# A decoder trunk on one core: layer 0's gates, sums and outputs stored by blocks of 128 tokens, and queries and keys asked for earlier in the code

## The chip, the cores and the metric

The kernel runs on one core of a Trainium2 chip. The metric is device time in microseconds (us): the median of several runs of the whole program. The engines are named as in the profile: PE (matrix multiply), DVE, ACT and POOL (elementwise work), and SP, which here only issues DMAs. SP and POOL each issue theirs in order from one queue, and the DMAs move data between DRAM and the core's SBUF.

## What is computed

Two transformer layers over one sequence of 2048 tokens of width 1024, in float32. Layer 0 has 16 heads, 8 of multi-head latent attention (MLA) and 8 of forgetting attention (FoX); both are causal softmax attention over all earlier tokens. Layer 1 is sliding-window attention and is not touched. Cut to what matters here:

```python
def even_mixer(x, w_in, ..., w_out, pos):
    h = x @ w_in
    cq, ckv, k_pe, fq, fk, fv, f_logit, gate = _split(h, EVEN_SIZES)
    ...
    o = jnp.concatenate([_merge(o_mla), _merge(o_fox)], axis=-1)
    return (o * jax.nn.silu(gate)) @ w_out

x = layer_norm(ALPHA * x + even_mixer(x, ...), ln_g, ln_b)
```

The kernel divides by the softmax sum late: attention leaves an undivided output, and the reciprocal of the sum of each head and token is multiplied in together with the gate.

## The kernel before, in words

Products keep float32 accuracy by splitting each operand into a high and a low part (`split_ps` L74, `split_sb` L78) and multiplying three times (`mm3` L85). The program is written with a tile library: each engine's order comes from its scheduler, which may place an instruction earlier than the code does, as soon as the buffer that it writes comes free. A buffer pool with `bufs=2` hands out two buffers in turn.

**Phase 1** (L186) computes layer 0's projections for four chunks of 512 tokens. `feature_tile` makes the SiLU gate, 128 channels by 512 tokens at a time, and stores it into `g1` in DRAM (L352), laid out as channel by token. Queries, keys and values go to DRAM as well.

**Phase 2** (L483) walks 16 heads by 4 chunks of queries, MLA and FoX in turn. `produce` (L509) loads the queries of one head and chunk (tiles `q0`, `q1`, pool `qpool`, two buffers; L519 to L528), multiplies them with the keys `ka` and `kb` that `load_head` (L457) brought, and takes the exponentials into `p`. It stores the reciprocal sums into `rd`, laid out as head by token (L565). `consume` (L567) transposes `p` on PE, splits it, multiplies by the values and stores the head's 64 rows into `og1[c]` (L591). The main loop (L667) interleaves `produce` of one step with `consume` of the step before. In the last step `prefetch` (L638) loads what layer 0's output product needs first: weights, the attention outputs of token blocks 0 and 1, and their gates and reciprocal sums, both blocks in one piece (L649). POOL multiplies them (L652, L654).

**Phase 3** (L778) makes the output product, the residual and the norm, one block of 128 tokens at a time, 16 blocks. `load_og` (L794) prepares a block:

```python
gt, rb = (bits(v[:]) for v in hl)            # the two tiles that later hold the split parts oh, ol
load_gate(gt, rb, t * 128, 128)
og = opool.tile([128, KB, 128], F32, name="og", bufs=1)
nc.sync.dma_start(out=og[:], in_=og1[t // 4][:, :, tok(t % 4)])
nc.gpsimd.tensor_tensor(out=og[:], in0=og[:], in1=gt, op=OP.mult)
nc.vector.tensor_tensor(out=og[:], in0=og[:], in1=rb, op=OP.mult)
return split_og(og[:], hl)
```

`load_gate` (L477) brings the gate (512 KB, into `oh`) and, for even and odd heads apart, the reciprocal sums (256 KB each, into `ol`), each copied out to 64 partitions. The tile `og` has one buffer, `oh` and `ol` have three each, and the residual tile `z` has five. `out_block` (L718) multiplies a prepared block on PE (48 matmuls into `py`, L727 to L729), adds the residual, and after every second block queues a norm (`finish` L766: ACT L768, then L771 and L772 on POOL for the first block and on DVE for the second, then the store to `x1` from POOL's queue). Near the end of phase 3 layer 1's first input is turned on PE (L146) and split (L76).

Of the kernel before, what the change touches and what calls it, by code (L numbers as in the profile page):

```python
# [17 lines left out]
T = 2048  # L18
# [21 lines left out]
def decoder_trunk(ctx, tc, x, x_t, w_lat, w_main, w_u, g_lat, b_f, w_out1, ln1,  # L40
# [20 lines left out]
    rd = dram.tile([16, T], F32, name="rd")  # L61
    g1 = dram.tile([D, T], F32, name="g1")
    og1 = [dram.tile([128, KB, 512], F32, name=f"og1_{c}") for c in range(4)]
# [7 lines left out]
    def bits(ap):  # L71
        return ap.bitcast(F32)
# [113 lines left out]
    def phase1(late):  # L186
# [145 lines left out]
        def feature_tile(n, m, chunk, xT, w):  # L332
# [14 lines left out]
            else:  # L347
# [4 lines left out]
                queue.dma_start(out=g1[p * 128:(p + 1) * 128, tcs], in_=sg[:])  # L352
# [124 lines left out]
    def load_gate(gt, rb, t0, n):  # L477

        nc.sync.dma_start(out=gt, in_=g1[:, t0:t0 + n].rearrange("(k p) t -> p k t", p=128))
        for s_ in range(2):  # L480
            nc.sync.dma_start(out=rb[s_ * 64:s_ * 64 + 64], in_=rd[:].rearrange("(k s) t -> s k t", s=2)[s_:s_ + 1, :, t0:t0 + n].broadcast_to([64, KB, n]))

    def phase2(ctx, kpool):  # L483
# [24 lines left out]

        def produce(n, c, st):  # L509
# [9 lines left out]
            q0 = qpool.tile([128, 512], F32R, name="q0")  # L519
            if mla:  # L520
                q1 = qpool.tile([128, 512], F32R, name="q1")
                for i, q in enumerate((q0, q1)):
                    nc.sync.dma_start(out=bits(q[0:64, :]), in_=qn[i][h, :, tcs])
                    for s_ in range(2):
                        nc.sync.dma_start(out=bits(q[64 + s_ * 16:80 + s_ * 16, :]), in_=qr[i][s_][h, :, tcs])
            else:
                nc.sync.dma_start(out=bits(q0[0:64, :]), in_=qf[0][h, :, tcs])
                nc.sync.dma_start(out=bits(q0[64:128, :]), in_=qf[1][h, :, tcs])  # L528
# [36 lines left out]
            nc.sync.dma_start(out=rd[h if mla else 8 + h, tcs].rearrange("(j p) -> p j", p=128), in_=rec[:])  # L565

        def consume(n, c, P):  # L567
# [18 lines left out]
            def finish(po):  # L586
                t2 = qpool.tile([64, 512], F32, name="t2")
                nc.scalar.copy(out=t2[:], in_=po[64:128, :])
                nc.vector.tensor_tensor(out=t2[:], in0=po[0:64, :], in1=t2[:], op=OP.add)  # L589
                queue = nc.gpsimd if (n, c) == (15, 3) else nc.sync  # L590
                queue.dma_start(out=og1[c][(hd % 2) * 64:(hd % 2) * 64 + 64, hd // 2, :], in_=t2[:])  # L591
# [45 lines left out]

        def prefetch():  # L638
# [9 lines left out]
            gts, rbs = (ppool.tile([128, T], F32, name="p")[:].rearrange("p (k q) -> p k q", k=KB) for _ in range(2))  # L648
            load_gate(gts, rbs, 0, 256)  # L649
            for t in range(2):  # L650
                nc.sync.dma_start(out=wout["og"][t], in_=og1[0][:, :, tok(t)])
            nc.gpsimd.tensor_tensor(out=gts, in0=gts, in1=rbs, op=OP.mult)  # L652
            for t in range(2):
                nc.gpsimd.tensor_tensor(out=wout["og"][t], in0=wout["og"][t], in1=gts[:, :, tok(t)], op=OP.mult)  # L654
            for steps, k, tag in ((PRE[0], 7, "vv"), (PRE[1], 4, "ka"), (PRE[2], 6, "kb")):
                for _ in range(steps):
                    yield 1
                wo_split(k, tag, raw[k], True)
            for _ in range(99):
                yield 1  # L660
# [6 lines left out]
        for n, c in todo + [(None, None)]:  # L667
            st = []
            gens = []
            if (n, c) == (15, 3):  # L670
                r3, r5 = wo_load(kpool.tile([128, T], F32, name="cb"), 3, 5)
            if n is None:
# [105 lines left out]
    def phase3(stack4, kpool, wout):  # L778
        with ExitStack() as ctx:
# [14 lines left out]
            def load_og(t):  # L794
                hl = parts()
                gt, rb = (bits(v[:]) for v in hl)
                load_gate(gt, rb, t * 128, 128)
                og = opool.tile([128, KB, 128], F32, name="og", bufs=1)
                nc.sync.dma_start(out=og[:], in_=og1[t // 4][:, :, tok(t % 4)])
# [462 lines left out]
```

## Time and profile before

| | us |
|---|---|
| three runs | 2655.42, 2666.89, 2667.24 |
| their median | 2666.89 |
| the profiled execution, its own time | 2674.29 |
| its span, first to last instruction | 2672.5 |
| PE busy in it | 2471.1 (92%) |
| DVE, ACT, POOL busy | 1531.1, 1172.7, 707.0 |

The profile is of one execution. A busy time says how long an engine had work in hand, not whether that work was on the path that sets the end. So it is read with the chain of work that ended last, with the waits of PE, and with windows: the same columns for one stretch of the span at a time, so that a stage stands by itself.

### The profile page before, as it was taken

To read this page: it belongs to the slowest core of one execution; us is meant where nothing else is said; L and a number is where in the kernel's file an instruction comes from. 1 tells how busy PE (TensorE), PEld (TensorE's weight loads), DVE (VectorE), ACT (ScalarE), POOL (GpSimd) and SP (SyncE) were. 2 spreads that over 40 slices of the span, in tenths; PEclk is the share of its full clock that TensorE was granted. 3 is DMA by queue.
4 is the path that set the end of the run, shared out by engine and by line. 5 is a ranking of instruction groups with operands and counts; after the bars stand their busy time and mean duration, and the time that the engine had idled before them with its cause. 6 is when DMAs were issued, how large, how long until landed. Compare 5 with 4: busy or idle time off the path is not lost.

```text
span 2672.5 us, 36349 instructions
## 1 busy us (share of the span) xinstructions
PE 2471.1 (92%) x12885; PEld 2050.3 (77%) x12885; DVE 1531.1 (57%) x3002; ACT 1172.7 (44%) x2409; POOL 707.0 (26%) x694
## 2 busy tenths in 40 slices
PE   8999999999999999999999787659999999999997
PEld 7898888987788887888877665437888887777775
DVE  5442264317787877777777643345633644777775
ACT  3121222217676866777676501011121115566663
POOL 2010011101222221222222333232321321356555
PEclk9999999999999999999999888879999999999998
DMA  6574346654556665454554558854444653566563
GB/s 204 177 251 143 106 152 235 202 167 62 95 93 93 83 114 86 83 111 79 97 84 83 115 151 170 151 129 156 142 138 141 177 154 100 150 150 165 155 155 103
DMA packets 298566, 360.91 MB, mean 135 GB/s; under 512 B 55920, under 2 KB 202352, under 8 KB 293776
## 3 DMA queue, kind: packets, MB, share of 16 engines
q1 hardware_dynamic: 294224, 343.51, 53.6%
q0 software_dynamic: 4160, 15.08, 1.5%
q8 instruction: 102, 1.67, 0.3%
q14 instruction: 80, 0.66, 0.2%
HBM read 240.20 MB, written 118.29 MB: 134 GB/s over the span
## 4 chain that ended last, share of the span: by engine, by line
PE 68%; DMA 17%; DVE 5%; POOL 3%; ACT 3%; issue 3%; SPq 1%; POOLq 0%; DVEq 0%; ACTq 0%
PE pm L91 11%; PE pm L89 11%; PE pm L90 10%; PE pt L604 6%; DMA og<-og 5%; PE S L547 4%; PE S L548 4%; PE po L581 3%; PE po L582 3%; DMA kb<-kf 3%; DMA q<-qr 3%; DMA q<-qf 2%; PE S L1061 2%; PE py L727 2%; PE S L550 2%
## 5 line engine op out<-in xcount | busy, mean ns | idle before, releaser
L76 DVE TENSOR_TENSOR tl<-pt,th 128x512 fp32r<-128x512 f32 (+3 forms) x672 | 400.7, 611 | 128.4 <-ACT th L75 125.2
L89 PE MATMUL pm<-xh,w 128*128 128x512 f32 x1088 | 428.7, 394 | 7.5 <-DVE z L734 5.6
L75 ACT CAST th<-pt 128x512 fp32r<-128x512 f32 (+3 forms) x672 | 340.4, 524 | 203.2 <-PE pt L604 168.1
L91 PE MATMUL pm<-xh,w 128*128 128x512 f32 x1088 | 425.9, 392 | 0.0
L90 PE MATMUL pm<-xl,w 128*128 128x512 f32 x1088 | 425.6, 391 | 0.0
L604 PE MATMUL pt<-ident,p 128*128 128x128 f32 x2176 | 348.0, 280 | 4.0 <-DVE tl L76 3.9
L561 ACT ACTIVATE p<-p,mx 128x128 f32<-128x128 f32 (+15 forms) x256 | 309.0, 1207 | 29.3 <-DVE mx L558 27.5
L604 PEld LDWEIGHTS pt<-ident,p 128*128 128x128 f32 x2176 | 271.8, 145 | 58.6 <-DVE tl L76 7.3
L547 PE MATMUL S<-ka,q 96*128 96x512 f32 (+5 forms) x640 | 253.4, 396 | 29.6 <-DMA q<-qf 11.5
L581 PE MATMUL po<-th,vv 128*128 128x512 f32 (+2 forms) x640 | 278.0, 434 | 0.6 <-DVE t L589 0.4
L82 POOL TENSOR_SCALAR w<-w_raw 128x1024 fp32r<-128x1024 f32 (+3 forms) x88 | 98.5, 1132 | 581.3 <-PE pm L91 418.8
L89 PEld LDWEIGHTS pm<-xh,w 128*128 128x128 f32 x1088 | 205.0, 188 | 49.5 <-issue 7.3
L582 PE MATMUL po<-tl,vv 128*128 128x512 f32 (+2 forms) x640 | 238.3, 373 | 0.0
L91 PEld LDWEIGHTS pm<-xh,w 128*128 128x128 f32 x1088 | 204.7, 188 | 42.9
L90 PEld LDWEIGHTS pm<-xl,w 128*128 128x128 f32 x1088 | 204.9, 188 | 41.6
L609 POOL TENSOR_SCALAR th<-tf 128x512 fp32r<-128x512 f32 x96 | 59.4, 618 | 668.8 <-ACT tf L608 363.8
L548 PE MATMUL S<-kb,q 96*128 96x512 f32 (+5 forms) x640 | 234.4, 369 | 0.0
L83 DVE TENSOR_TENSOR w<-w_raw,w 128x1024 fp32r<-128x1024 f32 (+3 forms) x89 | 138.6, 1572 | 130.4 <-POOL w L82 127.4
L558 DVE CUSTOM_DVE_ANT_0 p<-S,zm 128x1024 f32<-128x1024 f32 (+7 forms) x128 | 123.7, 967 | 104.4 <-PE S L550 103.4
L547 PEld LDWEIGHTS S<-ka,q 128*128 128x128 f32 (+1 forms) x640 | 124.5, 194 | 54.5 <-issue 23.3
L1062 DVE CUSTOM_DVE_ANT_0 p<-S,bm,nsk 128x256 f32<-128x256 f32 x256 | 117.7, 477 | 71.8 <-PE S L1061 69.7
L1064 ACT ACTIVATE p<-p,mx 128x256 f32<-128x256 f32 x256 | 129.0, 505 | 66.2 <-DVE mx L1062 65.7
(249 smaller groups left out, 4771.0 us busy)
## 6 DMA issues: line engine op xcount, KB each, us to landing
w_raw<-in_w_main_dram SPq DMA_DIRECT2D x40, 512.0 KB, 5.2
w_raw<-in_w_odd_dram SPq DMA_DIRECT2D x36, 512.0 KB, 4.5
vd<-s_v SPq DMA_DIRECT2D x64, 256.0 KB, 2.7
vv<-vd SPq DMA_DIRECT2D x16, 1024.0 KB, 10.6
qs<-hl SPq DMA_DIRECT2D x64, 256.0 KB, 3.5
qt<-qs SPq DMA_DIRECT2D x64, 256.0 KB, 5.3
ka<-kf SPq DMA_DIRECT2D x16, 512.0 KB, 9.4
kb<-kf SPq DMA_DIRECT2D x16, 512.0 KB, 9.0
```

The lines of the kernel that those rows point to most:

```text
L75: nc.scalar.copy(out=hi, in_=src)
L76: nc.vector.tensor_tensor(out=lo, in0=src, in1=bits(hi), op=OP.subtract)
L83: nc.vector.tensor_tensor(out=lo, in0=src, in1=bits(hi), op=OP.subtract)
L89: nc.tensor.matmul(ps, lhsT=ah, rhs=bh, start=(i == 0), stop=False)
L90: nc.tensor.matmul(ps, lhsT=ah, rhs=bl, start=False, stop=False)
L91: nc.tensor.matmul(ps, lhsT=al, rhs=bh, start=False, stop=(i == n - 1))
L547: nc.tensor.matmul(dst, lhsT=q0[ds, js], rhs=ka[ds, ks_], start=True, stop=False)
L548: nc.tensor.matmul(dst, lhsT=q0[ds, js], rhs=kb_[ds, ks_], start=False, stop=not (mla or diag))
L561: nc.scalar.activation(out=p[:, 0:L], in_=p[:, 0:L], func=AF.Exp, scale=-1.0, bias=acc[:], accum_out=su[:, j:j + 1])
L581: nc.tensor.matmul(po[0][:, q_:512], lhsT=vv[:, kb, :], rhs=th[:, k, q_:512], start=(kb == 0), stop=False)
L582: nc.tensor.matmul(po[0][:, q_:512], lhsT=vv[:, kb, :], rhs=tl[:, k, q_:512], start=False, stop=(kb == c * 4 + 3))
L604: nc.tensor.transpose(out=pt[:, k, :], in_=P[j][:, kk:kk + 128], identity=ident[:])
```

## The change

The layouts of `rd`, `g1` and `og1` in DRAM become block by block: all that a block of 128 tokens needs lies together, 4 KB in a row for each partition (for `rd`, 4 KB for the even heads and 4 KB for the odd heads). Stores into them become runs of 512 bytes where `g1` and `og1` had runs of 2 KB. `load_gate` loads one block. The gates and sums of token block 0 are asked for before the last step, into two new tiles `early`, and `prefetch` multiplies on DVE, where POOL did it before. The query loads move into `load_q` and are written one chunk ahead, and `load_head` is written while the second chunk of the head before is at work. Pools and their numbers of buffers stay as they are.

```diff
-    rd = dram.tile([16, T], F32, name="rd")
-    g1 = dram.tile([D, T], F32, name="g1")
-    og1 = [dram.tile([128, KB, 512], F32, name=f"og1_{c}") for c in range(4)]
+    rd = dram.tile([NB, 2, KB, 128], F32, name="rd")
+    g1 = dram.tile([NB, 128, KB, 128], F32, name="g1")
+    og1 = [dram.tile([4, 128, KB, 128], F32, name=f"og1_{c}") for c in range(4)]
...
-                queue.dma_start(out=g1[p * 128:(p + 1) * 128, tcs], in_=sg[:])
+                queue.dma_start(out=g1[chunk * 4:chunk * 4 + 4, :, p, :].rearrange("j p t -> p j t"), in_=sg[:].rearrange("p (j t) -> p j t", j=4))
...
-    def load_gate(gt, rb, t0, n):
-        nc.sync.dma_start(out=gt, in_=g1[:, t0:t0 + n].rearrange("(k p) t -> p k t", p=128))
+    def load_gate(gt, rb, t):
+        nc.sync.dma_start(out=gt, in_=g1[t])
         for s_ in range(2):
-            nc.sync.dma_start(out=rb[s_ * 64:s_ * 64 + 64], in_=rd[:].rearrange("(k s) t -> s k t", s=2)[s_:s_ + 1, :, t0:t0 + n].broadcast_to([64, KB, n]))
+            nc.sync.dma_start(out=rb[s_ * 64:s_ * 64 + 64], in_=rd[t, s_:s_ + 1].broadcast_to([64, KB, 128]))
...
+        queries = {}
+        def load_q(n, c):
...
+            if (n, c) not in queries:
+                queries[n, c] = load_q(n, c)
+            q0, q1 = queries.pop((n, c))
+            after = (n, c + 1) if c < 3 else (n + 1, 0)
+            if after[0] < 16:
+                queries[after] = load_q(*after)
+            if c == 1 and n + 1 < 16:
+                heads[n + 1] = load_head(kpool, n + 1)
...
-            nc.sync.dma_start(out=rd[h if mla else 8 + h, tcs].rearrange("(j p) -> p j", p=128), in_=rec[:])
+            hd = h if mla else 8 + h
+            nc.sync.dma_start(out=rd[c * 4:c * 4 + 4, hd % 2, hd // 2, :].rearrange("j p -> p j"), in_=rec[:])
...
-                queue.dma_start(out=og1[c][(hd % 2) * 64:(hd % 2) * 64 + 64, hd // 2, :], in_=t2[:])
+                queue.dma_start(out=og1[c][:, (hd % 2) * 64:(hd % 2) * 64 + 64, hd // 2, :].rearrange("j p t -> p j t"), in_=t2[:].rearrange("p (j t) -> p j t", j=4))
...
-            gts, rbs = (ppool.tile([128, T], F32, name="p")[:].rearrange("p (k q) -> p k q", k=KB) for _ in range(2))
-            load_gate(gts, rbs, 0, 256)
+            gates = [early, [v.rearrange("p (k q) -> p k q", q=128) for v in halves(ppool.tile([128, T], F32, name="p")[:])]]
+            load_gate(*gates[1], 1)
             for t in range(2):
-                nc.sync.dma_start(out=wout["og"][t], in_=og1[0][:, :, tok(t)])
-            nc.gpsimd.tensor_tensor(out=gts, in0=gts, in1=rbs, op=OP.mult)
-            for t in range(2):
-                nc.gpsimd.tensor_tensor(out=wout["og"][t], in0=wout["og"][t], in1=gts[:, :, tok(t)], op=OP.mult)
+                nc.sync.dma_start(out=wout["og"][t], in_=og1[0][t])
...
+            for t in range(2):
+                for v in gates[t]:
+                    tc.keep_in_program_order(nc.vector.tensor_tensor(out=wout["og"][t], in0=wout["og"][t], in1=v, op=OP.mult))
...
             if (n, c) == (15, 3):
                 r3, r5 = wo_load(kpool.tile([128, T], F32, name="cb"), 3, 5)
+                early = [pool.tile([128, KB, 128], F32, name=f"early{i}")[:] for i in range(2)]
+                load_gate(*early, 0)
...
-                load_gate(gt, rb, t * 128, 128)
+                load_gate(gt, rb, t)
-                nc.sync.dma_start(out=og[:], in_=og1[t // 4][:, :, tok(t % 4)])
+                nc.sync.dma_start(out=og[:], in_=og1[t // 4][t % 4])
```

How the change moves instructions is shown for three places. In rows of the order a name with a number is one tile; tile numbers and line numbers differ between the two programs.

SP's queue at the first FoX head of phase 2, where its first query load stands (`qf` is the FoX queries in DRAM, `qr` and `qn` those of MLA), before:

```order
L565 DMA rd<-rec 128x4x1
L525 DMA q_5111<-qr_72 16x512
L527 DMA q_5332<-qf_77 64x512
L528 DMA q_5332<-qf_78 64x512
L523 DMA q_5965<-qn_68 64x512
```

and now:

```order
L582 DMA rd<-rec 128x4x1
L524 DMA q_4978<-qr_71 16x512
L524 DMA q_4978<-qr_72 16x512
L518 DMA q_5128<-qf_77 64x512
L518 DMA q_5128<-qf_78 64x512
L522 DMA q_5773<-qn_68 64x512
```

The query loads stand where they stood, but for this one store of `rec`, which is one place earlier; over the whole of phase 2 the queue holds the same loads and stores in the same order, apart from three added loads of `early`.

SP's queue in the last head, where the second of the two added loads of sums stands (the first stands two heads earlier, likewise behind a store of `rec` and ahead of a query load), before:

```order
L527 DMA q_14781<-qf_77 64x512
L528 DMA q_14781<-qf_78 64x512
L591 DMA og_2_88<-t_14611 64x512
L565 DMA rd<-rec 128x4x1
L527 DMA q_14934<-qf_77 64x512
L528 DMA q_14934<-qf_78 64x512
```

and now:

```order
L518 DMA q_14703<-qf_77 64x512
L518 DMA q_14703<-qf_78 64x512
L608 DMA og_2_88<-t_14614 64x4x128
L582 DMA rd<-rec 128x4x1
L481 DMA early_14938<-rd 64x1024
L518 DMA q_14784<-qf_77 64x512
L518 DMA q_14784<-qf_78 64x512
```

The load of `early` reads what the store of `rec` just ahead of it writes, and the query load of the last step is now behind it.

DVE at the end of phase 2 and the start of phase 3 (`tl` are the splits of the last transposed `p`, `t` the last head's output, `cb` the attention outputs of token blocks 0 and 1, `ol` their low parts), before:

```order
L76 TENSOR_TENSOR tl<-pt,th 128x4x128 x3
L76 TENSOR_TENSOR tl<-pt,th 128x128
L76 TENSOR_TENSOR tl<-pt,th 128x2x128
L76 TENSOR_TENSOR tl<-pt,th 128x3x128
L76 TENSOR_TENSOR tl<-pt,th 128x4x128
L589 TENSOR_TENSOR t_15339<-po,t_15339 64x512
L83 TENSOR_TENSOR ol<-cb,oh 128x1024
```

and now:

```order
L76 TENSOR_TENSOR tl<-pt,th 128x4x128 x2
L678 TENSOR_TENSOR cb<-cb,early_14937 128x1024
L76 TENSOR_TENSOR tl<-pt,th 128x4x128
L678 TENSOR_TENSOR cb<-cb,early_14938 128x1024
L678 TENSOR_TENSOR cb<-cb,p 128x1024
L76 TENSOR_TENSOR tl<-pt,th 128x128
L678 TENSOR_TENSOR cb<-cb,p 128x1024
L76 TENSOR_TENSOR tl<-pt,th 128x2x128
L76 TENSOR_TENSOR tl<-pt,th 128x3x128
L76 TENSOR_TENSOR tl<-pt,th 128x4x128
L606 TENSOR_TENSOR t_15344<-po,t_15344 64x512
L83 TENSOR_TENSOR ol<-cb,oh 128x1024
```

Four multiplications of 128x1024 stand among the last splits, and POOL's three (L652, L654) are gone. Phase 3's rows are in the same order on every engine.

## Rows read from the trace of the kernel before

**Rows 1.** Page, part 4: the chain that ended last, shares by engine.

```profile
PE 68%; DMA 17%; DVE 5%; POOL 3%; ACT 3%; issue 3%; SPq 1%; POOLq 0%; DVEq 0%; ACTq 0%
```

**Rows 2.** Windows: stretch, length, engines' busy us (instructions), granted PE clock, DMA share, GB/s.

```profile
590.00:1500.00 910.00, 866.01 (x5125) 726.47 (x5124) 682.39 (x1426) 650.81 (x1202) 200.21 (x315) 0.97 0.54 88
1500.00:1545.00 45.00, 24.76 (x118) 20.08 (x117) 20.32 (x24) 15.13 (x25) 19.18 (x15) 0.73 0.71 143
1545.00:1845.00 300.00, 207.24 (x797) 160.61 (x796) 126.21 (x144) 38.28 (x40) 95.47 (x74) 0.84 0.66 149
```

**Rows 3.** Waits of PE, 1500 to 1845: us in total, times, longest us.

```profile
PE py L727 <- POOL oh L82: 17.1, 1, 17.1
PE py L727 <- ACT oh L80: 70.6, 12, 12.3
PE pt L146 <- DVE xl L76: 12.8, 1, 12.8
```

**Rows 4.** Chain that ended last, in time: start us, us, what.

```profile
1503.45 25.32 DMA p<-rd
...
1546.60 15.66 DMA og<-og
...
1594.85 2.38 POOL og L800
...
1600.96 16.27 DMA og<-og
...
1822.55 1.23 DVE ol L83
```

**Rows 5.** Page's DMA issues, all lines: count, KB each, median us to landing.

```profile
z<-in_x_dram SPq DMA_DIRECT2D x16, 512.0 KB, 5.3
gt<-g SPq DMA_DIRECT2D x16, 512.0 KB, 4.9
rb<-rs SPq DMA_DIRECT2D x64, 128.0 KB, 4.0
og<-t SPq DMA_DIRECT2D x63, 128.0 KB, 4.6
g<-s_x SPq DMA_DIRECT2D x31, 256.0 KB, 3.6
ol<-rd SPq DMA_DIRECT2D x28, 256.0 KB, 14.5
og<-og SPq DMA_DIRECT2D x14, 512.0 KB, 14.6
rd<-rec SPq DMA_DIRECT2D x64, 2.0 KB, 11.3
```

**Rows 6.** Windows of 3 us at the start of phase 3 (columns as in rows 2).

```profile
1546.00:1549.00 3.00, 3.00 (x14) 2.34 (x13) 1.45 (x3) 0.00 (x0) 0.00 (x0) 1.00 0.95 302
1555.00:1558.00 3.00, 3.00 (x15) 2.50 (x14) 0.00 (x0) 0.00 (x0) 0.00 (x0) 1.00 0.13 41
```

**Rows 7.** Timeline of SP and POOL, 1702 to 1715.

```profile
1702.44 0.54 SPq L799 DMA_DIRECT2D og<-og  x1
1712.22 2.41 POOL L800 TENSOR_TENSOR og<-og,oh 128x1024 f32<-128x1024 f32 x1
```

**Rows 8.** Timeline of PE: first and last matmul of half a block, 24 in all.

```profile
1557.21 0.39 PE L727 MATMUL py<-ka,oh 128*128 128x512 f32 x1
1562.43 0.39 PE L729 MATMUL py<-wo_hi,ol 128*128 128x512 f32 x1
```

**Rows 9.** Waits of PE, 590 to 1500 (columns as in rows 3).

```profile
PE S L550 <- DMA q<-qr: 13.0, 7, 2.9
PE S L547 <- DMA q<-qf: 11.5, 6, 2.7
```

**Rows 10.** Timeline of SP, 1458 to 1474.

```profile
1461.05 0.38 SPq L565 DMA_DIRECT2D rd<-rec  x1
1469.38 0.45 SPq L527 DMA_DIRECT2D q<-qf  x1
```

More of the change, by code (lines that the diff above doesn't have):

```diff
@@ L507, in cuts @@
             return [(s0, w, 128 if w % 512 == 128 and w > 512 else 0) for s0, w in parts]
+        queries = {}
+        def load_q(n, c):
+            h = n // 2
+            tcs = slice(c * 512, (c + 1) * 512)
+            q0 = qpool.tile([128, 512], F32R, name="q0")
+            if n % 2:
+                for i in range(2):
+                    nc.sync.dma_start(out=bits(q0[i * 64:i * 64 + 64, :]), in_=qf[i][h, :, tcs])
+                return q0, None
+            q1 = qpool.tile([128, 512], F32R, name="q1")
+            for i, q in enumerate((q0, q1)):
+                nc.sync.dma_start(out=bits(q[0:64, :]), in_=qn[i][h, :, tcs])
+                for s_ in range(2):
+                    nc.sync.dma_start(out=bits(q[64 + s_ * 16:80 + s_ * 16, :]), in_=qr[i][s_][h, :, tcs])
+            return q0, q1
         def produce(n, c, st):
@@ L518, in produce @@
             tcs = slice(c * 512, (c + 1) * 512)
[L519 to L528, printed above, removed]
+            if (n, c) not in queries:
[6 more added lines that the diff above has]
+                heads[n + 1] = load_head(kpool, n + 1)
             su = sm.tile([128, 4], F32, name="su")
@@ L636, in wo_split, with halves @@
             wout[k] = (v[:, 0:D], v[:, D:T])
+        def halves(t):
+            return t[:, 0:D], t[:, D:T]
         def prefetch():
```

## The prediction

> **What bounds the kernel now.** I read the chain that ended last first: PE carries 68% of it and DMA 17%, so transfers are on the path somewhere [rows 1]. The windows say where. Through phase 2 PE is busy 866 of 910 us, but from 1545 to 1845, which is phase 3, it is busy 207 of 300 us, at a mean granted clock of 0.84 of its higher level, and around the change of phase (1500 to 1545) 25 of 45 us [rows 2]. The list of PE's waits names the prepared block: 17.1 us for the first `oh`, then 70.6 us in 12 waits for the later ones [rows 3]. So about 88 us of waiting for prepared blocks can be had, and a little more from the clock; that is the stage that the layouts touch.
>
> How a block gets prepared is read from the chain in order of time. `og` has one buffer, so its load goes out only when the block before is split, and every step is load, POOL, DVE, ACT, DVE. From POOL's start at 1594.85 to the next load's issue at 1600.96 are 6.1 us; that load then took 16.3 us [rows 4]. The loads of the 14 blocks of phase 3 run from 1546.60 to the last split's end at 1823.8 [rows 4]: 277.2 us, **19.8 us a step**. PE needs less: 24 matmuls in 23 intervals of (1562.43 - 1557.21) / 23 = 0.227 us, so 48 take 10.9 us [rows 8].
>
> Why does the load take 15 us? The median landing of `og` is 14.6 us, and `gt`, as large and read in the same runs of 512 bytes in layer 1, lands in 4.9 us [rows 5]. So it is not the runs of 512 bytes. What stands ahead of `og` in the queue is the pair of `ol<-rd` loads, 256 KB each, 14.5 us [rows 5]. While they run alone the queue moves 41 GB/s with only 0.13 of the DMA engines busy, and just before, while the norm's weights (4 KB in a row, copied out to 128 partitions) load, it moves 302 GB/s [rows 6]. 512 KB at 41 GB/s are 12.8 us. The load `p<-rd` shows the same rate: 2 x 512 KB in 25.3 us are 41 GB/s too, in runs of 1 KB [rows 4]. What these two share is the source: eight rows, two heads apart (16 KB), read by 64 partitions at once. So I read them as bound by where the source lies, neither by its bytes nor by its packets.
>
> **The change, part by part.**
>
> Sums by block. The source becomes 4 KB in a row, as the norm's weights are. Bounds for 512 KB: 12.8 us if nothing changes, 1.7 us at the 302 GB/s. I take the fast end, because a load of the same shape ran there, and layer 1's `rb` (2 KB in a row, 64 partitions) lands in 4.0 us [rows 5]. The Trainium skill ("DMA: Bandwidth & Descriptors", latency and other measured facts) has an entry on row pitches that are large powers of two: 512 KiB still ran at full rate and only 2 MiB and more lost. By that entry a pitch of 16 KB costs nothing, the cause would be the copying out itself, and the new layout would not help; that is rival 1.
>
> Gates and outputs by block. `oh<-g` and `og` get runs of 4 KB for 512 bytes. From 4.9 (`gt`) to 5.3 us (`z`, runs of 4 KB) [rows 5] this alone is worth nothing.
>
> The step in phase 3. With the queue ahead of it empty, `og` lands after 4.9 us at best and 10 at worst (an `oh`, `ol` and `z` of 1.5 MB at 302 GB/s in front of it: 5 us more). I take 6.0: those were mostly issued a step earlier. A plain step is then 6.0 + 6.1 = 12.1 us. Before every second block POOL first does a norm: 9.8 us pass from `og`'s issue at 1702.44 to POOL's multiplication at 1712.22 [rows 7]; the load is hidden in them, and the step is 9.8 + 6.1 = 15.9 us. Six of the 14 steps are of that kind (the blocks 4, 6, ... 14): 8 x 12.1 + 6 x 15.9 = 192 us. The turning of layer 1's input, now hidden in the waits, will show in part; its one wait is 12.8 us [rows 3], I add 5 (0 to 12.8). 197 against 277: **80 us less**. POOL's norm is what is late next.
>
> The start of phase 3. The first `oh` waited for `p<-rd` until 1528.8, then for POOL. Block 0's gates and sums are now there long before, block 1's are half as large and fast. Of the 17.1 us [rows 3] I expect 14 back: the four DVE multiplications, some 1.2 us each, stand among the last splits, and one of them fills a gap there; about 3 us are left. Bounds: 5 (the loads of `og` late) to 17. POOL's removed three were the wait itself and are counted in it.
>
> Queries and keys ahead. Zero. SP's queue has them where it had them, since the pool still has two buffers and the scheduler already placed each load at the moment its buffer came free. The waits on query loads (13.0 and 11.5 us are the largest) [rows 9] stay.
>
> The early loads. Each reads `rd` right behind a store into it, which lands after 11.3 us [rows 5], and the queue stands until then. In the last head the store went out at 1461.05, so it stands to about 1472.4, and the query load that went at 1469.38 goes 3 us later [rows 10]; it is for a step that starts some 10 us on. Twice 0 to 3 us; I take 1 in all.
>
> Stores in runs of 512 bytes. `g1`: 32 of 256 KB, landing in 3.6 us; `og1`: 64 of 128 KB, in 4.6 us [rows 5]. No row shows such a store. The bounds are nothing (`gt` shows that reading in such runs costs nothing) and the slowest rate in the trace, 41 GB/s: 6.4 and 3.2 us of transfer. I take nothing, by the nearer row; three buffers for the gate tile cover it, with a product every 24 x 0.227 = 5.4 us.
>
> **Sum.** 80 + 14 - 1 = 93 us. Against the profiled execution's own 2674.3 that gives 2581. It lies 7.4 us above the median of the three runs, so against the median I forecast 2667 - 93 = **2574 us**.
>
> **The rivals.**
>
> 1. Copying one source out to 64 partitions is slow wherever it lies. Then `ol` stays at 12.8 us a step and phase 3 at 19.8; only the start gains, with the sums of one block there early and those of the other half as large: some 15 to 25 us, 2645 us. For it: both slow loads copy out. Against it: so do the two fast ones. The Trainium skill's entry on pitches, above, points this way.
> 2. POOL's norm does not hold up the chain, because the blocks can be prepared ahead. Then PE sets the pace: 14 x 10.9 = 153 us, 124 less than now, plus 14: 2535 us if nothing else holds it, about 2545 with the turning. Against it: one `og` buffer, and POOL's order is as it was.
> 3. Slower: the stores in short runs go at 41 GB/s. From about 5.4 us for a gate tile on (the product's own pace) SP's queue falls behind; with 6.4 us the 16 stores of each half take 102 us and four weights of 1 MB at 302 GB/s 14 us, against 16 x 5.4 = 87 us of products: 29 us late a half, some 60 in all. In phase 2 3.2 us would stand ahead of query loads in 64 steps, where PE already waits for them: up to 64 x 2 = 128 us. Less 93 of gain, and it comes out about 2760, 95 slower; it takes half of that to lose all the gain. Against it: the stores of 2 KB runs land fast at pitches of 8 and 16 KB.
> 4. The loads written ahead do act, and PE's query waits go [rows 9]: 25 us more, 2549 us. The order speaks against it.
>
> **How the numbers follow.** Forecast 0.70, rival 1 0.12, rival 2 0.11, rival 3 0.04, rival 4 0.03. About 0.5% (13 us) is what a measurement of this kernel can tell from no change. The forecast's own bounds: `og` at 4.9 us and the turning free take 14 off, the whole 17 us at the start 3; `og` at 10 us adds 8 x 4 = 32, the turning 8, the start 9. That is 2557 to 2623. To hold 8 in 10 I go to 2546 below, which takes in rival 4 and most of rival 2, and to 2630 above. Faster: the forecast, rivals 2 and 4 and most of rival 1, 0.93; same 0.04; slower 0.03.
>
> **What would show it.** Right: `ol<-rd` lands in about 5 us, no window of phase 3 stays near 41 GB/s, `og` near 6; PE's wait for the first `oh` falls to some 3 us and the 70.6 us to 15 or 20; the steps alternate between 12 and 16 us, with POOL's L772 ahead of every second `og`. PE's waits on query loads as before. Wrong: `ol` still above 12 us (rival 1); even steps near 11 us (rival 2); weights or queries late in phases 1 and 2, with `g` or `og` stores above 6 us (rival 3); the query waits gone (rival 4).

## The result and the profile after

| | before | after |
|---|---|---|
| median, us (runs) | 2666.0 (4) | 2916.93 (4) |
| range, us | 2655.42 to 2667.24 | 2900.04 to 2934.98 |
| ratio to before, 95% interval | 1 | 1.0949 (1.0917 to 1.0981) |

The change makes the kernel 9.5% slower, where 3.5% faster was forecast. Phase 3 gained about what was forecast, and the passage into it less. Phase 2, which the prediction had at plus 1 us, grew by 307 us.

The timeline groups the instructions of an engine on one tile: engine, line, operation, tiles, count, shortest, median and longest duration in ns, and the starts of the first and the last. Three such rows and the span, 2898.3 us, cut the program after the change into stages:

```profile
L563 PE MATMUL S<-ka,q x640: 276/397/796, 595.2 to 1799.7; 96*128 96x512 f32 x56, 128*128 128x512 f32 x56, 96*128 96x384 f32 x16, 128*128 128x384 f32 x16
L749 PE MATMUL py<-wo_hi,oh x320: 387/393/795, 1843.9 to 2889.7; 128*128 128x512 f32 x160
L822 POOL TENSOR_TENSOR og<-og,oh x14: 2350/2384/2404, 1852.0 to 2038.7; 128x1024 f32<-128x1024 f32 x14
```

The same rows of the kernel before:

```profile
L547 PE MATMUL S<-ka,q x640: 276/394/776, 598.0 to 1495.2; 96*128 96x512 f32 x56, 128*128 128x512 f32 x56, 96*128 96x384 f32 x16, 128*128 128x384 f32 x16
L727 PE MATMUL py<-wo_hi,oh x320: 387/394/793, 1545.8 to 2663.7; 128*128 128x512 f32 x160
L800 POOL TENSOR_TENSOR og<-og,oh x14: 2327/2356/2407, 1562.3 to 1817.8; 128x1024 f32<-128x1024 f32 x14
```

`S` holds the scores, so its first and last product mark phase 2; the first `py` is the start of phase 3, and POOL's last `og` is the last block prepared in it.

| stage | before, us | after, us | difference |
|---|---|---|---|
| to the first product of the scores | 598.0 | 595.2 | -2.8 |
| phase 2: first to last product of the scores | 897.2 | 1204.5 | +307.3 |
| from there to phase 3's first product | 50.6 | 44.2 | -6.4 |
| phase 3: to POOL's last `og` | 272.0 | 194.8 | -77.2 |
| the rest | 854.7 | 859.6 | +4.9 |

Phase 1 is untouched by its new stores of `g1`; phase 3 and its start gained 84 us; phase 2 lost 307 us.

**Phase 2.** The windows (stretch, length, busy us of PE, PEld, DVE, ACT and POOL with counts, granted PE clock, DMA share, GB/s), after:

```profile
590.00:1800.00 1210.00, 924.00 (x5083) 767.96 (x5081) 683.21 (x1418) 647.15 (x1196) 199.99 (x314) 0.86 0.61 67
1800.00:1844.00 44.00, 32.10 (x150) 24.88 (x149) 26.21 (x36) 19.26 (x31) 11.69 (x14) 0.84 0.71 144
1844.00:2045.00 201.00, 163.58 (x677) 128.75 (x676) 109.78 (x118) 33.14 (x34) 85.04 (x64) 0.92 0.66 209
```

Against [rows 2], PE was idle for 286 us of phase 2 instead of 44, and the same products kept it busy 58 us longer: its granted clock fell from 0.97 to 0.86 of the higher level in a stage with many pauses. The DMA engines were busier (0.61 for 0.54) and moved less in the same time (67 GB/s for 88), while the bytes of the stretch stayed the same (some 81 and 80 MB): the transfers took longer, there were no more of them to move. PE's waits from 590 to 1815 (us in total, times, longest) name the loads of the queries, and `t`, the tile of a head's output, which comes free when its store into `og1` has landed:

```profile
PE S L563 <- DMA q<-qf: 83.8, 8, 17.2
PE S L566 <- DMA q<-qr: 71.7, 16, 11.4
PE po L598 <- DVE t L606: 39.4, 6, 14.2
PE S L563 <- DMA q<-qr: 34.5, 5, 9.1
...
PE S L563 <- DMA kb<-kf: 10.8, 2, 6.0
```

Before, the two query waits were 11.5 and 13.0 us [rows 9]. These loads are the victims. SP's queue waits longest for engines that finish the tile that it is to store, before as after (L608 for `t` 201.8 us, before 155.5); its waits for other transfers in the same stretch point at who held the loads up (L481 is the load of the early sums, L524 and L518 are query loads, L582 the store of `rec`, L474 the load of a head's decays):

```profile
SPq L474 <- DMA og<-t: 52.0, 6, 14.2
...
SPq L524 <- DMA rd<-rec: 40.2, 9, 13.1
...
SPq L481 <- DMA rd<-rec: 34.3, 2, 21.0
SPq L582 <- DMA rd<-rec: 34.3, 6, 11.1
...
SPq L518 <- DMA og<-t: 17.1, 4, 8.3
```

The waits for `rec` before, 590 to 1500 (L525 and L523 load queries, L565 is the store):

```profile
SPq L525 <- DMA rd<-rec: 7.6, 4, 2.6
SPq L523 <- DMA rd<-rec: 7.4, 5, 2.0
...
SPq L565 <- DMA rd<-rec: 5.4, 4, 2.6
```

Two stores stand there, `rec` into `rd` and `t` into `og1`, and the change gave both a new layout. The chain that ended last shows them in time (start us, us, what):

```profile
1019.22 16.64 DMA rd<-rec
1035.87 13.70 DMA kb<-kf
1049.59 14.86 DMA q<-qr
...
1068.09 18.60 DMA q<-qr
...
1160.47 27.23 DMA og<-t
...
1197.66 18.11 DMA kb<-kf
1215.78 16.01 DMA q<-qr
```

And the chain's shares moved from PE to DMA, from 68% and 17% [rows 1] to:

```profile
PE 59%; DMA 26%; DVE 4%; POOL 3%; ACT 3%; issue 3%; SPq 1%; another core or an unknown queue 1%; DVEq 0%; POOLq 0%; ACTq 0%
```

**Phase 3.** PE's waits for prepared blocks, 1800 to 2060, against 17.1 and 70.6 us [rows 3]:

```profile
PE pt L146 <- DVE xl L76: 14.6, 1, 14.6
PE py L749 <- ACT oh L80: 11.3, 7, 3.9
PE py L749 <- POOL oh L82: 1.1, 1, 1.1
```

One pair of steps in the chain, against the single step of [rows 4]:

```profile
1858.06 5.37 DMA og<-og
1863.56 2.39 POOL og L822
...
1872.09 2.42 POOL z L793
1874.57 3.25 POOL z L794
...
1878.79 2.41 POOL og L822
...
1886.38 5.59 DMA og<-og
1892.13 2.40 POOL og L822
```

The load of `og` takes 5.4 and 5.6 us where it took 16. From one `og` on POOL to the next are 15.2 us with POOL's norm (`z`) between them and 13.3 without; over the next six they are 15.9 to 16.9 and 11.1 to 13.7. No window crawls at 41 GB/s [rows 6] any more: a pair of `ol<-rd` that goes out behind its `oh` at 1851.72 has landed 4.0 us later (the chain again), and the window in between moves 272 GB/s:

```profile
1851.72 4.02 DMA ol<-rd
```

```profile
1852.00:1855.00 3.00, 3.00 (x15) 2.49 (x14) 1.61 (x4) 0.00 (x0) 2.38 (x1) 1.00 0.91 272
```

### The profile page after: what moved, and what is told of

Read it like the earlier page. It is cut to its first block, busy times and chain, and to the rows that moved or that the text cites. A ratio compares the mean times of both kernels' runs of the same rounds, so it can differ in the third digit from the quotient of the medians.

```text
span 2898.3 us, 36360 instructions
## 1 busy us (share of the span) xinstructions
PE 2519.4 (87%) x12885; PEld 2086.9 (72%) x12885; DVE 1539.8 (53%) x3006; ACT 1173.6 (40%) x2409; POOL 698.4 (24%) x691
## 4 chain that ended last, share of the span: by engine, by line
PE 59%; DMA 26%; DVE 4%; POOL 3%; ACT 3%; issue 3%; SPq 1%; another core or an unknown queue 1%; DVEq 0%; POOLq 0%; ACTq 0%
PE pm L89 10%; PE pm L91 10%; PE pm L90 10%; DMA q<-qr 9%; DMA q<-qf 5%; PE pt L621 4%; DMA kb<-kf 4%; DMA og<-t 3%; PE S L563 3%; PE S L564 2%; PE po L598 2%; PE py L749 2%; PE S L1083 2%; PE py L751 2%; PE py L750 2%
## 5 line engine op out<-in xcount | busy, mean ns | idle before, releaser
L563 PE MATMUL S<-ka,q 96*128 96x512 f32 (+5 forms) x640 | 269.8, 422 | 154.0 <-DMA q<-qf 83.8
L621 PE MATMUL pt<-ident,p 128*128 128x128 f32 x2176 | 366.3, 290 | 27.7 <-DVE tl L76 19.7
L621 PEld LDWEIGHTS pt<-ident,p 128*128 128x128 f32 x2176 | 287.5, 151 | 88.2 <-DVE tl L76 23.9
L598 PE MATMUL po<-th,vv 128*128 128x512 f32 (+2 forms) x640 | 287.9, 450 | 42.3 <-DVE t L606 39.4
L563 PEld LDWEIGHTS S<-ka,q 128*128 128x128 f32 (+1 forms) x640 | 134.7, 210 | 182.7 <-issue 154.8
L564 PE MATMUL S<-kb,q 96*128 96x512 f32 (+5 forms) x640 | 248.2, 390 | 0.0
L599 PE MATMUL po<-tl,vv 128*128 128x512 f32 (+2 forms) x640 | 246.5, 385 | 0.7 <-DVE tl L76 0.7
L566 PE MATMUL S<-ka,q 96*128 96x512 f32 (+2 forms) x320 | 130.1, 408 | 71.7 <-DMA q<-qr 71.7
L574 DVE CUSTOM_DVE_ANT_0 p<-S,cb 128x1024 f32<-128x1024 f32 (+7 forms) x128 | 123.1, 966 | 111.4 <-PE S L564 100.6
```

The lines of the kernel that those rows point to most:

```text
L563: nc.tensor.matmul(dst, lhsT=q0[ds, js], rhs=ka[ds, ks_], start=True, stop=False)
L564: nc.tensor.matmul(dst, lhsT=q0[ds, js], rhs=kb_[ds, ks_], start=False, stop=not (mla or diag))
L574: nc.vector.tensor_tensor_reduce(out=p[:, s0:s0 + w], in0=S[:, b:b + w], in1=in1, op0=OP.add, op1=OP.min, scale=-scale, scalar=3e38 if acc ...
L598: nc.tensor.matmul(po[0][:, q_:512], lhsT=vv[:, kb, :], rhs=th[:, k, q_:512], start=(kb == 0), stop=False)
L599: nc.tensor.matmul(po[0][:, q_:512], lhsT=vv[:, kb, :], rhs=tl[:, k, q_:512], start=False, stop=(kb == c * 4 + 3))
L621: nc.tensor.transpose(out=pt[:, k, :], in_=P[j][:, kk:kk + 128], identity=ident[:])
```

## The experiments

Every ratio is to the kernel before, measured on the same chip in the same batch. "Phase 2" is the time from the first to the last product of the scores, as in the table above.

**1. Which store? The sums back in their old layout.** One part of the change undone:

```diff
-    rd = dram.tile([NB, 2, KB, 128], F32, name="rd")
+    rd = dram.tile([16, T], F32, name="rd")
...
-            nc.sync.dma_start(out=rd[c * 4:c * 4 + 4, hd % 2, hd // 2, :].rearrange("j p -> p j"), in_=rec[:])
+            nc.sync.dma_start(out=rd[h if mla else 8 + h, tcs].rearrange("(j p) -> p j", p=128), in_=rec[:])
```

and the loads of `rd` to match.

> The change, but the reciprocal sums rd keep their old layout, stores and loads (g1 and og1 by block as in the change). Theory S (the stores of rec into rd by block, four runs of 512 bytes in elements of 4 bytes, hold up what stands behind them in SP's queue): phase 2 (from 597 us to the last products of the scores) goes back from about 1218 to 905 to 930 us and PE's waits on q, kb and t fall back to about 40 us; the loads of ol from rd are slow again, some 14 us, so phase 3 takes about 270 us as before; the time is 2640 to 2680 us. Theory O (the 512-byte runs of the og1 stores do it): phase 2 stays near 1200 us, phase 3 is slow as well, about 2960 us. Theory B (each bears a part): in between.

Measured: 2657.15 us, ratio 0.9973 (0.9933 to 1.0013), phase 2 of 900.2 us. Theory S, and with `rd` out, all that is left of the change is within the noise of no change. One part of the expectation missed: phase 3 did not stay near 270 us. From its first product to POOL's last `og` it took 253.9 us, where the table has 272.0 for the kernel before, so another part of the change shortens it; experiment 8 finds which.

**2. The outputs back in their old layout.**

```diff
-    og1 = [dram.tile([4, 128, KB, 128], F32, name=f"og1_{c}") for c in range(4)]
+    og1 = [dram.tile([128, KB, 512], F32, name=f"og1_{c}") for c in range(4)]
```

with the store and the two loads to match.

> The change, but the outputs og1 keep their old layout (runs of 2 KB in the stores, of 512 bytes in the loads); rd and g1 by block. Theory S (stores of rec): phase 2 stays near 1200 us, the loads of ol stay fast, 2880 to 2930 us. Theory O (stores of og1): phase 2 goes back to some 910 us and phase 3 keeps its gain, about 2580 to 2600 us.

Measured: 2926.74 us, ratio 1.0962 (1.0852 to 1.1073), phase 2 of 1235.3 us. The waits on `og<-t` were effects: this store stood in the same trouble as the loads.

**3. The sums' new layout alone, in the kernel before.**

```diff
-    rd = dram.tile([16, T], F32, name="rd")
+    rd = dram.tile([NB, 2, KB, 128], F32, name="rd")
```

with its store, and its loads block by block.

> The kernel before with rd by block alone (stores of rec and loads of the sums; the sums of blocks 0 and 1 in two loads each; everything else as before). Theory S: phase 2 grows from 910 to about 1200 us, phase 3 gets 60 to 80 us shorter, 2860 to 2920 us. Theory O: phase 2 stays at 910 us, phase 3 gets shorter, about 2590 us.

Measured: 2904.67 us, ratio 1.088 (1.0839 to 1.092), phase 2 of 1201.8 us. One layout, written by stores of 2 KB, carries the whole loss. Phase 3 is 201.5 us for 272.0, 70.5 us shorter by the sums alone.

**4. The same four pieces, at another pitch.** A store of `rec` writes four runs of 512 bytes, one for each block, in elements of 4 bytes; 128 partitions write four elements each. Before, the four runs lay one behind the other. In the change they lie 8192 bytes apart. Only that distance is altered:

```diff
-    rd = dram.tile([NB, 2, KB, 128], F32, name="rd")
+    rdp = dram.tile([NB, 2 * KB * 128 + 128], F32, name="rd")
+    rd = rdp[:, 0:2 * KB * 128].rearrange("b (s k t) -> b s k t", s=2, k=KB)
```

> The change, with the block pitch of rd padded from 8192 to 8704 bytes and nothing else: the four runs of 512 bytes of a store of rec no longer lie a power of two apart. Theory S with the pitch as its cause: phase 2 falls to some 905 to 950 us, 2575 to 2620 us in all. Theory S without it (that the store is in four pieces, or that they lie where the heads' pieces lie side by side, is enough) and theory O: no change, 2880 to 2930 us.

Measured: 2622.88 us, ratio 0.9824 (0.9785 to 0.9863), phase 2 of 926.4 us. Adding 512 bytes of nothing to each block turns 9.5% slower into 1.8% faster. So it is neither the four pieces nor the small elements alone, but where the pieces lie. Phase 2 came out within the range given for it, the time 3 us above its range.

**5. The small elements gone.** With the block layout and the pitch of 8192 bytes as in the change, `rec` is turned on PE, so that a store is four rows of 512 bytes:

```diff
-            nc.sync.dma_start(out=rd[c * 4:c * 4 + 4, hd % 2, hd // 2, :].rearrange("j p -> p j"), in_=rec[:])
+            recs[n, c] = rec
...
+            pt = ps_t.tile([128, 4, 128], F32, name="pt")
+            nc.tensor.transpose(out=pt[0:4, 0, :], in_=recs.pop((n, c))[:], identity=ident[:])
+            rt = fpool.tile([4, 128], F32, name="rt")
+            nc.scalar.copy(out=rt[:], in_=pt[0:4, 0, :])
+            nc.sync.dma_start(out=rd[c * 4:c * 4 + 4, hd % 2, hd // 2, :], in_=rt[:])
```

The added lines stand at the start of `consume`.

> The change, with its block layout of rd as it is (pitch 8192 bytes), but each rec is turned on PE at the start of the next step and copied by ACT, so that its store is 4 pieces of 512 bytes instead of 512 of 4 bytes. If it is the stores in elements of 4 bytes that are slow, and not the layout: phase 2 (first to last product of the scores) at about 900 us or a little below, the loads of the sums fast, 2575 to 2600 us, the fastest kernel so far. If any write at this pitch is slow: phase 2 stays above 1000 us. If the 64 turnings and copies cost PE and ACT more than the waits on the queue: some 2625 us, as the padded layout.

Measured: 2554.69 us, ratio 0.9579 (0.9548 to 0.9609), phase 2 of 868.1 us: 4.2% faster than before, with its twins in experiments 7 and 12 the fastest kernel of this study, and 20 us under the range given for it. Its windows of phase 2, of the start of phase 3, and of phase 3:

```profile
590.00:1465.00 875.00, 853.80 (x5152) 712.06 (x5151) 674.48 (x1418) 658.37 (x1259) 200.04 (x314) 1.00 0.35 92
1465.00:1500.00 35.00, 28.88 (x152) 22.34 (x151) 28.87 (x37) 19.43 (x32) 12.86 (x14) 0.95 0.59 190
1500.00:1700.00 200.00, 162.98 (x679) 128.54 (x678) 107.54 (x118) 33.52 (x34) 85.66 (x64) 0.92 0.66 209
```

Phase 2 now has PE busy 854 of 875 us at a granted clock of 1.00, and the DMA share falls to 0.35 (0.54 in [rows 2]) at the same bytes. All that is left of its waits:

```profile
PE S L563 <- DVE mx L574: 16.8, 35, 0.9
PE S L566 <- DMA q<-qr: 2.8, 1, 2.8
```

The price of turning is 64 small products on PE and 64 copies on ACT (the line's own view and that of the tile `rt`; shortest, median, longest in ns):

```profile
L610 PE MATMUL pt<-ident,rec x64: 269/272/377, 604.3 to 1471.0; 128*4 128x128 f32 x64
```

```profile
L612 ACT COPY rt<-pt x64: 238/255/258, 604.7 to 1471.5; 4x128 f32<-4x128 f32 x64
```

That is 17 us of PE (64 x 0.272) and 16 us of ACT, less than the waits that went. That phase 2 got shorter than the kernel before's, 897 us, says that the old stores had a price too; experiment 6 measures it.

**6. Turning alone, in the kernel before.** The same lines, with `rd` as it was: `out=rd[hd, tcs].rearrange("(j p) -> j p", p=128)`.

> The kernel before, rd in its old layout, with each rec turned on PE and stored as four rows of 512 bytes instead of 512 elements of 4 bytes. If the small stores already cost the kernel before what separates its phase 2 (897 us from first to last product of the scores) from the turned version of the change (868 us): 2630 to 2645 us, phase 3 as before. If that gain came from the queries and keys asked for ahead, which only then have room to act: 2660 to 2670 us.

Measured: 2630.78 us, ratio 0.9853 (0.9825 to 0.988), phase 2 of 866.0 us. Its window of phase 2, against 866.01 us busy of 910 at a clock of 0.97 [rows 2]:

```profile
590.00:1463.00 873.00, 854.07 (x5152) 712.27 (x5151) 673.86 (x1417) 657.46 (x1259) 199.15 (x314) 1.00 0.34 91
```

So the stores in small elements, with their runs side by side, cost the kernel before 38 us more than turning does (2668.59 in this batch less 2630.78), and the rest of the change is worth 76 us on top of it (2630.78 less 2554.69).

**7. Queries and keys not ahead.** From the version of experiment 5, back to the old place in the code:

```diff
-            if (n, c) not in queries:
-                queries[n, c] = load_q(n, c)
-            q0, q1 = queries.pop((n, c))
...
+            q0, q1 = load_q(n, c)
```

> The turned version of the change with queries and keys written where the kernel before has them (no chunk and no head ahead); layouts and the early sums as in the change. If asking ahead does nothing, since the order of SP's queue is the same: 2550 to 2560 us, phase 2 at 868 us. If it acts now that the stores are out of the way: 2565 to 2580 us, with PE's waits on q some 10 us or more.

Measured: 2553.42 us, ratio 0.9565 (0.9531 to 0.9599), phase 2 of 868.8 us. Asking ahead is worth nothing without slow stores. With them no run isolates it; experiment 3, which has the slow stores and does not ask ahead, took 2904.67 us for the change's 2916.93, so no gain shows there either.

**8. Gates and outputs back, the sums by block.** From experiment 5, `g1` and `og1` as in the kernel before.

> The turned version of the change with gates and outputs (g1, og1) in their old layout, so that only rd lies by block. If the gain of phase 3 is the sums' alone, as the prediction had it (runs of 512 bytes cost the loads nothing): 2550 to 2565 us, POOL's first to last og multiplication of phase 3 at 187 us as in the change. If the 4 KB runs of og and oh carry part of it: 2570 us or more, that stretch above 195 us.

Measured: 2564.05 us, ratio 0.9602 (0.9575 to 0.9628), phase 2 of 868.4 us, POOL's stretch of `og` 195.2 us against 186.3. Most of the gain is the sums', but not all: the block layout of gates and outputs gives some 9 us in that stretch, and 11 in the time against experiment 7, of the same batch. Phase 2 is the same with either layout (868.4 and 868.1 us), so it is the loads that gain. The time fell inside the range for one answer and the stretch for the other.

**9. The store from another queue.**

```diff
-            nc.sync.dma_start(out=rd[c * 4:c * 4 + 4, hd % 2, hd // 2, :].rearrange("j p -> p j"), in_=rec[:])
+            nc.scalar.dma_start(out=rd[c * 4:c * 4 + 4, hd % 2, hd // 2, :].rearrange("j p -> p j"), in_=rec[:])
```

> The change, its stores of rec into rd unchanged in form and pitch (8192 bytes), but issued from ACT's queue, where nothing else of phase 2 goes. If a slow store only holds up what stands behind it in the same queue: the query and key loads are free again, phase 2 at 900 to 930 us, about 2580 to 2620 us. If it takes the DMA engines or the memory that all queues share: phase 2 stays above 1100 us, about 2850 us or more.

Measured: 2881.29 us, ratio 1.0801 (1.0756 to 1.0845), phase 2 of 1181.1 us, 23 less than the change's. Another queue saves 36 us of 250: the second answer. SP's queue still waits for these stores, which are no longer in it (590 to 1790; L522 loads queries, L481 the early sums, L470 a head's values):

```profile
SPq L522 <- DMA rd<-rec: 82.1, 13, 13.8
SPq L481 <- DMA rd<-rec: 43.9, 2, 29.9
...
SPq L470 <- DMA rd<-rec: 39.7, 5, 9.8
```

The Trainium skill ("DMA: Bandwidth & Descriptors", issuing engines are not separate DMA queues) says that DMAs of every issuing engine run on the same 16 DMA engines. 36 us of gain for a queue of its own fits that, but does not show it, because SP also waited for the landing of these stores. L481 reads what they write, so its wait is a true one; L522 and L470 read nothing of it, and why they wait was not taken apart.

**10. What about the place? Pitches.** With experiment 4's edit, at five other pitches: 12288, 8448, 9216, 8320 and 16384 bytes (rows of `rdp` of 3072, 2112, 2304, 2080 and 4096 elements).

> The change with rd's block pitch at 12288 bytes, three times 4096. If only powers of two are slow: about 2620 us, as with 8704 bytes. If every multiple of 4096 (or 2048) bytes is: about 2900 us, as with 8192; in between if the four pieces share some of what they write to.

> The change with rd's block pitch at 8448 bytes (8192 and 256). With 8704 phase 2 was still 29 us longer than before. If that rest depends on the pitch, it differs here by 10 us or more; if it comes from the store being in four pieces at all, or from another part of the change, phase 2 takes about 926 us again and the time is about 2620 us.

> The change with rd's block pitch at 9216 bytes (8192 and 1024). Theory P (what counts is how many different places of 512 bytes modulo 8192 a store covers): four places, as with 8704, so phase 2 at 900 to 940 us and 2600 to 2635 us in all. Theory R (no such period): anything else, above 2650 us for instance.

> The change with rd's block pitch at 8320 bytes (8192 and 128): the four pieces cover 896 bytes modulo 8192. Theory P: between the 2917 us of 8192 bytes and the 2800 us of 8448, so 2830 to 2900 us. Theory R: outside of these.

> The change with rd's block pitch at 16384 bytes. Theory P: one place modulo 8192, as in the change, 2900 to 2935 us. Theory R: it differs from the change by more than 40 us to either side.

| pitch, bytes | offsets of the four runs modulo 8192 | phase 2, us | time, us | ratio (95%) |
|---|---|---|---|---|
| 512 (old layout, experiment 1) | 0, 512, 1024, 1536 | 900.2 | 2657.15 | 0.9973 (0.9933 to 1.0013) |
| 9216 | 0, 1024, 2048, 3072 | 903.3 | 2603.35 | 0.9736 (0.9679 to 0.9793) |
| 8704 | 0, 512, 1024, 1536 | 926.4 | 2622.88 | 0.9824 (0.9785 to 0.9863) |
| 12288 | 0, 4096, 0, 4096 | 1020.5 | 2715.81 | 1.018 (1.0135 to 1.0226) |
| 8448 | 0, 256, 512, 768 | 1105.5 | 2800.2 | 1.0497 (1.0453 to 1.054) |
| 8320 | 0, 128, 256, 384 | 1242.1 | 2936.36 | 1.0982 (1.0892 to 1.1072) |
| 16384 | 0, 0, 0, 0 | not compared | 2898.84 (one run) | none |
| 8192 (the change) | 0, 0, 0, 0 | 1204.5 | 2916.93 | 1.0949 (1.0917 to 1.0981) |

A second run at 16384 bytes took 2956.19 us, 57 us longer, and the profile is of that one, so its phase 2 is left out; 2898.84 us is 18 from the change and 1 under the range of theory P. Theory P was written down when 8704, 12288, 8448 and 8192 bytes had been measured, so the other three pitches test it: 9216 bytes came out as it wanted, 16384 close to it, and 8320 did not (it wanted 2830 to 2900 us, and the kernel is as slow as the change). In its own terms 12288 and 8448 bytes stand the wrong way round too: the four runs cover 1024 bytes modulo 8192 at 12288 and 1280 at 8448, and 8448 is the slower. What fits all rows with a phase 2 afterwards is to count only where the runs start, in units of 512 bytes modulo 8192: four different places for 512, 9216 and 8704 bytes (phase 2 of 900 to 926 us), two for 12288 and 8448 (1020 and 1105 us), one for 8320 and 8192 (1242 and 1204 us). That is an ordering that these pitches suggest, made after the fact and with 26 to 85 us between rows of one group; it is not a mechanism that was shown.

**11. One run at a time.** Four DMAs for each `rec`, each 128 elements into one run:

```diff
-            nc.sync.dma_start(out=rd[c * 4:c * 4 + 4, hd % 2, hd // 2, :].rearrange("j p -> p j"), in_=rec[:])
+            for j in range(4):
+                nc.sync.dma_start(out=rd[c * 4 + j, hd % 2, hd // 2, :].rearrange("(p o) -> p o", o=1), in_=rec[:, j:j + 1])
```

> The change, but each rec is stored by four DMAs, one for each block of 128 tokens, each 128 elements of 4 bytes into one run of 512 bytes; layout and pitch as in the change. If what is slow is one DMA that writes small elements in turn into four places 8 KB apart: phase 2 at 900 to 960 us, 2580 to 2640 us. If small elements into these places are slow in any order: phase 2 near 1200 us, about 2900 us; the 192 more DMAs alone could cost up to 30 us on SP's queue in either case.

Measured: 3448.97 us, ratio 1.2916 (1.2842 to 1.2991), phase 2 of 1741.8 us, 537 us more than the change's. Neither answer foresaw this. The pieces written one after the other are the worst of all; how much of it is the small elements in one place and how much the 192 more DMAs, the run doesn't part. PE's waits in its phase 2:

```profile
PE S L563 <- DMA q<-qr: 201.5, 14, 29.0
PE S L566 <- DMA q<-qr: 187.5, 11, 24.2
PE po L599 <- DVE t L607: 136.5, 7, 32.7
```

**12. Small elements, spread.** The version of experiment 5 with one more store of `rec` in every step, 512 elements of 4 bytes, 64 bytes apart, into a tile that nothing reads:

```diff
+            nc.sync.dma_start(out=probe[n, c].rearrange("(j p o) -> o p j", p=128, o=16)[0], in_=rec[:])
```

> The turned version of the change, to which each step adds one more store of rec into a DRAM tile of its own that nothing reads, its 512 elements 64 bytes apart (32 KB in all for each store). If the place alone makes small elements dear (theory P), a store spread over all places costs little: 2555 to 2575 us. If 512 elements of 4 bytes cost some 29 us over the 64 stores wherever they go, as the old stores did in the kernel before: 2580 to 2595 us. If every element now opens a new place and that is dear: above 2620 us.

Measured: 2551.87 us, ratio 0.9544 (0.9492 to 0.9596), phase 2 of 869.7 us. Sixty-four stores with as many small elements as those of the change cost nothing that can be seen, just under theory P's range. They stand where the change's stores of `rec` stood in the code, so it was not the later place of the store that made experiment 5 faster. The four elements of one partition also lie 8192 bytes apart here, as in the change (128 elements of 64 bytes), so that distance by itself is not dear. But each element has 64 bytes to itself, where sixteen elements of `rec` share as many in `rd`, and nothing reads the tile; so this run does not tell apart many places from no neighbours.

The Trainium skill ("DMA: Bandwidth & Descriptors", specifications) says that transfers under 512 bytes are read, altered and written back. It does not say that the price depends on where the bytes lie. Here 64 stores of as many elements cost nothing, 38 us (experiment 6) or 362 us (2916.93 for the change less the 2554.69 of experiment 5), by where the elements lie; the last two may be up to 17 us more, since the kernels that they are measured against pay for the turning.

## Why the prediction was wrong, point by point

**The step that failed is "Sums by block".** It priced the loads of `rd`, and the prediction put a price on the new stores of `g1` and `og1` under "Stores in runs of 512 bytes", but the third store that the layout changes, `rec` into `rd`, has no term in the sum. Its row was read: `rd<-rec`, 64 times, 2 KB each, 11.3 us to landing [rows 5], and it was used only for how long the early loads stand behind it. It moves the fewest bytes of the rows shown and lands later than most of them: either it stood behind others or its form made it slow, and the row alone cannot tell. Changing such a form without bounding it was the mistake. A bound was at hand: if what stands behind each of the 64 stores waited for a whole landing more, that is 64 x 11.3 = 723 us, an end that would have reached far past the result. What the runs showed in place of the missing term: 362 us over the kernel whose stores have no small elements (experiment 5), and 307 us of phase 2 over the kernel before, which had paid a part already.

**Phase 3: the mechanism right, the size in part by luck.** Forecast: 277 us to 197, 80 us less, all of it by the sums; measured 77 us less from the first product to POOL's last `og`. The seven plain steps took 11.1 to 14.7 us, 13.0 on average, for the forecast 12.1, the six with POOL's norm 15.2 to 16.9, 15.9 on average, for 15.9. POOL's norm is what is late next, as said. But the sums alone gave less than 80 us: 70.5 in experiment 3, and 62.8 from experiment 6 (268.4) to experiment 8 (205.6). The rest came from the gates and outputs, which had been put at nothing: a gain of the sums put 10 to 17 us too high and a gain of the others missed by 7 to 11 us, which offset each other.

**The start of phase 3: the wait right, the gain too high.** PE's wait for the first `oh` fell to 1.1 us (forecast 3). In the change only 6 us of the 14 came through, and what took the rest is not shown. In experiment 5 the stretch from the last score to the first `py` is 35.1 us (1464.9 to 1500.0) for 50.6, 15.5 less; but turning alone brings it to 44.7 (experiment 6), so 9.6 of them are the change's.

**Gates and outputs by block: "worth nothing" was 9 to 11 us short.** Experiment 8.

**Stores of `g1` and `og1` in runs of 512 bytes: nothing, right.** Phase 1 did not move, with `og1` as before the change stays as slow (experiment 2), and without the slow stores phase 2 takes 868.1 us with the short runs and 868.4 with the long ones (experiments 5 and 8).

**Queries and keys ahead: zero, right.** Experiment 7, and SP's order had said so.

**The early loads: 1 us forecast.** SP stood 34.3 us in two waits for `rd<-rec` (L481, above). They are a part of the same missing price: in experiment 5 the same two waits, for the turned store, are 1.7 us:

```profile
SPq L481 <- DMA rd<-rt: 1.7, 2, 0.8
```

**The sum without the missing term.** Forecast 93 us. Of the 112 us that experiment 5 gains (2667.02 in its batch less 2554.69) 38 are the old stores' own price, which no term had (experiment 6), and 76 the change's other parts (the two differences span two batches, hence 114). From the last score to the end, experiment 6's kernel takes 1165.6 us and experiment 5's 1086.7: 78.9 us less, 9.6 at the start and 73.7 to POOL's last `og`, with 4.4 given back later. So even without the slow stores the 93 us were some 15 too many.

**The rivals.** Rival 1 (copying out to 64 partitions is slow anyway) is out: the sums land in 4.0 us for 14.5 [rows 5]. The entry of the Trainium skill that it leaned on ("DMA: Bandwidth & Descriptors", latency and other measured facts) has pitches hurt from 2 MiB on and measured none below 512 KiB. Here loads from a pitch of 16 KB ran at 41 GB/s [rows 6], and stores at one of 8 KB cost 307 us. Its observation that a small pad doesn't help and a larger one does has its like in the table, at 128 and 512 bytes. What made the old loads slow stays open: the change took away the pitch and the short runs, each read by 64 partitions, together, and no run parts them. Rival 2 (even steps near 11 us) is out, rival 4 too. (The 2535 us of rival 2 is reckoned from the profiled execution; from the median it is 2667 - 124 - 14 = 2529.) Rival 3, the one that ended slower, had the sign and the victims (query loads behind stores in SP's queue) and named the wrong store; it had a chance of 0.04.

## What to carry to other kernels

When a layout in DRAM changes, cost each transfer that touches it, the stores with the loads, and start with those that move few bytes and land late: a store of 2 KB can outweigh loads of 512 KB. Elements of 4 bytes from many partitions into a few short runs are the form to avoid: a turn on PE (0.27 us) and a copy (0.26 us) made four full rows of 512 bytes of them and gave 38 us in the kernel before and 362 in the change. Where a small store must stay, try another pitch before anything else; 512 or 1024 bytes of padding gave back some 300 us here, 256 bytes 117 and 128 bytes nothing.

## What the runs showed that had not been expected

- The cost of a store in 4-byte elements goes by where its runs lie: with the same elements, in the same order and number, phase 2 took 900 us at a pitch of 512 bytes, 903 at 9216, 926 at 8704, 1020 at 12288, 1105 at 8448, 1204 at 8192 and 1242 at 8320; spread 64 bytes apart they cost nothing. Why the place counts is open.
- Writing the four runs by four DMAs instead of one made phase 2 1742 us long for 1204.
- The slow stores delayed loads of other data even when they were issued from another engine's queue (36 us of 250 came back).
- With PE waiting for loads in pauses of up to 17 us, its granted clock fell to 0.86 in phase 2; without these waits it was 1.00, and the same products took 854 us of busy time instead of 924.
